# Scaling 16384 tokens by two weights each: smaller tiles, four output buffers, and five of the stores in the ScalarE queue

## The chip, the core and the metric

The kernel runs on one core of a Trainium2 chip. Such a core has compute engines with instruction streams of their own; this kernel computes on VectorE (DVE in the profile) and ScalarE (ACT). SyncE (SP) computes nothing: its stream issues transfers. Data moves between the chip's memory (HBM) and the core's buffer (SBUF, 128 partitions) by 16 DMA engines. They serve two queues here: one is filled by SyncE's stream (q1 in the profile), the other by ScalarE's (q10). The metric is the device time of one execution in microseconds, the median of several runs.

## The reference

```python
batch, seq, hidden, n_experts = 16, 1024, 512, 8
k = 2
x_expanded = x[:, :, np.newaxis, :].repeat(k, axis=2)
weights = expert_weights[..., np.newaxis]
return (x_expanded * weights).astype(np.float32)
```

Every one of the 16 x 1024 = 16384 tokens is a row of 512 fp32 numbers (2 KB). It is written twice, each time multiplied by one of the token's two weights. So 33.6 MB of x are read, 67.1 MB are written, and each number written takes one multiplication. The indices of the experts are not used.

## The kernel before

The tokens are dealt in groups. A group of T tokens per partition takes T x 128 consecutive tokens, and each partition gets T consecutive ones of them (`rows`, L45), so a partition's part of a group is one contiguous piece of memory. `groups` is `[[24], [24], [24], [24], [24], [8]]`, in all the 128 tokens of each partition; each inner number is one tile of x. A tile of 24 tokens has 48 KB in each partition.

The weights come first, in three transfers in SyncE's queue: the first group (L53), the four other groups of 24 (L54), and the group of 8 (L58). A partition's weights of one group of 24 are 24 x 2 fp32 numbers, a row of 192 B; the group of 8 has rows of 64 B.

`load(i)` (L74) issues the load of tile i in ScalarE's queue (L82). The first tile comes in six pieces of 4 tokens (8 KB per partition), every other tile in one transfer. There are two x buffers, so tiles 0 and 1 are loaded ahead, and tile i + 2 is issued by ScalarE's stream after its multiplications of tile i (L119).

The main loop (L90) goes through the tiles, and in each through its tokens and the two weights. An output buffer holds 12 tokens with both copies (48 KB per partition), and there are two of them. Of the products, every third (`c % 3 == 2`) is made on ScalarE (L100), the others on VectorE (L106), each over 128 x 512 numbers, with the weight as one scalar per partition. After every 12 tokens, and at the end of a tile, the output buffer is stored by a transfer in SyncE's queue (L115). All eleven stores are in that queue.

The streams wait by semaphores that the framework sets: a multiplication waits for its tile of x and for the store that last used its output buffer, a store waits for the multiplications that fill its buffer, and a load waits for the multiplications that read its x buffer last. In one stream everything stands in the order of the program: in ScalarE's, the load of tile i + 2 stands between the multiplications of tiles i and i + 1.

Of the kernel before, what the change touches and what calls it, by code (L numbers as in the profile page):

```python
# [1 line left out]

# [4 lines left out]


@with_exitstack
def kernel(  # L10
    ctx: ExitStack,
    tc: tile.TileContext,
    x: bass.AP,
    expert_indices: bass.AP,
    expert_weights: bass.AP,
    out: bass.AP,
):
    nc = tc.nc

    batch, seq, hidden = x.shape  # L20
    k = expert_weights.shape[-1]
    P = nc.NUM_PARTITIONS
    ntok = batch * seq
    assert ntok % P == 0
    A_TOTAL = ntok // P

    f32 = mybir.dt.float32
    row = k * hidden
    TX = 24
    TO = 12  # L30

    groups = [[24], [24], [24], [24], [24], [8]]
    assert sum(sum(g) for g in groups) == A_TOTAL

    xf = x.rearrange("b s h -> (b s) h")
    of = out.rearrange("b s k h -> (b s) (k h)")
    wf = expert_weights.rearrange("b s k -> (b s) k")

    w_pool = ctx.enter_context(tc.tile_pool(name="w_pool", bufs=1))
    x_pool = ctx.enter_context(tc.tile_pool(name="x_pool", bufs=2))  # L40
    o_pool = ctx.enter_context(tc.tile_pool(name="o_pool", bufs=2))

    w_tile = w_pool.tile([P, A_TOTAL * k], f32)

    def rows(of_all, done, T):  # L45
        return of_all[done * P : (done + T) * P, :].rearrange(
            "(p a) n -> p (a n)", a=T
        )

    T0 = sum(groups[0])  # L50
    G = len([g for g in groups[1:] if sum(g) == T0])
    head = (1 + G) * T0
    nc.sync.dma_start(out=w_tile[:, : T0 * k], in_=rows(wf, 0, T0))  # L53
    nc.sync.dma_start(  # L54
        out=w_tile[:, T0 * k : head * k].rearrange("p (g n) -> p g n", g=G),
        in_=wf[T0 * P : head * P, :].rearrange("(g p a) n -> p g (a n)", g=G, p=P),
    )
    nc.sync.dma_start(  # L58
        out=w_tile[:, head * k :], in_=rows(wf, head, A_TOTAL - head)
    )  # L60

    tiles = []
    done = 0
    for group in groups:
        T = sum(group)
        a0 = 0
        for n in group:
            tiles.append((done, T, a0, n))
            a0 += n
        done += T  # L70

    loaded = []

    def load(i):  # L74
        if i >= len(tiles):
            return
        done, T, a0, n = tiles[i]
        x_tile = x_pool.tile([P, TX * hidden], f32)
        src = rows(xf, done, T)
        step = TX // 6 if i == 0 else n  # L80
        for at in range(0, n, step):
            nc.scalar.dma_start(  # L82
                out=x_tile[:, at * hidden : (at + step) * hidden],
                in_=src[:, (a0 + at) * hidden : (a0 + at + step) * hidden],
            )
        loaded.append(x_tile)

    for i in range(2):
        load(i)
    for i, (done, T, a0, n) in enumerate(tiles):  # L90
        x_tile = loaded[i]
        outr = rows(of, done, T)
        for t in range(n):
            if t % TO == 0:
                o_tile = o_pool.tile([P, TO * row], f32)
            for kk in range(k):
                c = (done + a0 + t) * k + kk
                o = t % TO * row + kk * hidden
                if c % 3 == 2:
                    nc.scalar.mul(  # L100
                        out=o_tile[:, o : o + hidden],
                        in_=x_tile[:, t * hidden : (t + 1) * hidden],
                        mul=w_tile[:, c : c + 1],
                    )
                    continue
                nc.vector.tensor_scalar(  # L106
                    out=o_tile[:, o : o + hidden],
                    in0=x_tile[:, t * hidden : (t + 1) * hidden],
                    scalar1=w_tile[:, c : c + 1],
                    scalar2=None,  # L110
                    op0=mybir.AluOpType.mult,
                )
            if (t + 1) % TO == 0 or t + 1 == n:
                at = t // TO * TO
                nc.sync.dma_start(  # L115
                    out=outr[:, (a0 + at) * row : (a0 + t + 1) * row],
                    in_=o_tile[:, : (t + 1 - at) * row],
                )
        load(i + 2)  # L119

# [1 line left out]
_INS = ['x', 'expert_indices', 'expert_weights']  # L122
_OUTS = [((16, 1024, 2, 512), 'float32')]


# [23 lines left out]
```

## Time and profile before

| what | value |
|---|---|
| time, median of 3 runs | 240.6 us (240.56 to 240.91) |
| span of the profiled execution | 238.9 us |
| read from HBM, written to it | 33.69 MB, 67.11 MB |
| load of 24 tokens: size, issue to landing | 6144 KB, 43.9 us (median of 4) |
| store of 12 tokens: size, issue to landing | 6144 KB, 33.6 us (median of 10) |
| one multiplication on VectorE, on ScalarE | 480 ns, 709 ns |

The span goes from the first to the last instruction of the profiled execution; the runs are timed from outside and take in what lies around it. The profile cuts the span in 40 slices; a digit in the row of an engine, or of the DMA engines, is the busy share of that slice in tenths, and 9 stands for 90% or more. A DMA queue's line gives its packets, its megabytes and the time of its packets as a share of the time of 16 engines. A packet is one contiguous row, here the part of one partition in one transfer, and 4 B packets mark the ends of transfers. Lines of waits give who waited for whom: the total in us, how many times, and the longest.

### The profile page before, as it was taken

What the parts mean: (1) busy time and instruction counts of PE and PEld (TensorE: products, weight loads), DVE (VectorE), ACT (ScalarE), POOL (GpSimd) and SP (SyncE); (2) the same over time, 40 slices, a digit from 0 to 9 for tenths busy, and PEclk for the clock granted to TensorE, in tenths of its full rate; (3) what the DMA queues carried; (4) which work ended last, traced back from release to release, by engine and by line L of the source; (5) the groups of instructions that cost most, each with busy time, mean ns of one, the idle gap of its engine ahead of it and who ended that gap; (6) DMA issues with size and microseconds to landing.
All of it is one profiled execution on the core that took longest, in us unless ns stands there. A gap on an engine that the chain in (4) does not pass through costs nothing.

```text
span 238.9 us, 364 instructions
## 1 busy us (share of the span) xinstructions
DVE 69.0 (29%) x171; ACT 54.9 (23%) x86; POOL 0.2 (0%) x4
## 2 busy tenths in 40 slices
DVE  0890300004609100190063037003706406415000
ACT  0870300004308000170071034003406106213000
POOL 0000000000000000000000000000000000000000
DMA  6999999999999999999999999999989899999994
GB/s 244 420 443 395 495 395 395 494 428 395 428 494 395 413 494 411 395 446 469 403 411 502 395 420 453 436 411 428 469 379 496 381 428 469 436 411 428 436 439 197
DMA packets 3986, 100.81 MB, mean 422 GB/s; under 512 B 1168, under 2 KB 1168, under 8 KB 1168
## 3 DMA queue, kind: packets, MB, share of 16 engines
q1 hardware_dynamic: 2400, 67.24, 65.2%
q10 hardware_dynamic: 1584, 33.56, 33.1%
q14 instruction: 2, 0.02, 0.0%
HBM read 33.69 MB, written 67.11 MB: 422 GB/s over the span
## 4 chain that ended last, share of the span: by engine, by line
DMA 66%; DVE 13%; another core or an unknown queue 11%; issue 0%; DVEq 0%; SPq 0%
DMA out_dram<-o_tile 54%; DVE o_tile L106 13%; DMA x_tile<-in_x_dram 11%; DVEq L144 0%; DVEq L106 0%; SPq L115 0%
## 5 line engine op out<-in xcount | busy, mean ns | idle before, releaser
L106 DVE TENSOR_SCALAR o_tile<-x_tile,w_tile 128x512 f32<-128x512 f32 x171 | 69.0, 480 | 149.3 <-DMA out_dram<-o_tile 105.3
L100 ACT ACTIVATE o_tile<-x_tile,w_tile 128x512 f32<-128x512 f32 x85 | 53.6, 709 | 155.5 <-DMA out_dram<-o_tile 116.8
L100 ACT ACT_TABLE_LOAD x1 | 1.3, 1283 | 6.7 <-DMA x_tile<-in_x_dram 6.7
L133 POOL MEMSET const-bfloat16-1.0<- 128x1 bf16 x1 | 0.1, 101 | 0.0
L133 POOL MEMSET const-uint8-127<- 128x1 uint8 x1 | 0.1, 101 | 0.0
L133 POOL MEMSET const-float32-0.0<- 128x1 f32 x1 | 0.1, 98 | 0.2 <-issue 0.2
L133 POOL MEMSET const-float32-1.0<- 128x1 f32 x1 | 0.1, 98 | 0.0
## 6 DMA issues: line engine op xcount, KB each, us to landing
out_dram<-o_tile SPq DMA_DIRECT2D x10, 6144.0 KB, 33.6
x_tile<-in_x_dram ACTq DMA_DIRECT2D x4, 6144.0 KB, 43.9
x_tile<-in_x_dram ACTq DMA_DIRECT2D x6, 1024.0 KB, 10.6
out_dram<-o_tile SPq DMA_DIRECT2D x1, 4096.0 KB, 19.5
x_tile<-in_x_dram ACTq DMA_DIRECT2D x1, 2048.0 KB, 24.0
w_tile<-in_expert_weights_dram SPq DMA_DIRECT2D x1, 96.0 KB, 11.1
w_tile<-in_expert_weights_dram SPq DMA_DIRECT2D x1, 24.0 KB, 2.9
w_tile<-in_expert_weights_dram SPq DMA_DIRECT2D x1, 8.0 KB, 13.2
```

What stands on the lines that cost most here:

```text
L100: nc.scalar.mul(out=o_tile[:, o : o + hidden], in_=x_tile[:, t * hidden : (t + 1) * hidden], mul=w_tile[:, c : c + 1],)
L106: nc.vector.tensor_scalar(out=o_tile[:, o : o + hidden], in0=x_tile[:, t * hidden : (t + 1) * hidden], scalar1=w_tile[:, c : c + 1], scala ...
L133: nc = _bacc.Bacc("TRN2", target_bir_lowering=False, num_devices=1)
```

## The change

- A tile of x has 16 tokens (32 KB per partition) in place of 24; there are still two x buffers. The first tile comes in four pieces of 4 tokens in place of six.
- An output buffer has 8 tokens (32 KB per partition) in place of 12, and there are four of them in place of two. So there are 16 pieces j = 0 to 15 of 8 tokens, and 16 stores in place of 11. The SBUF in use stays at 192 KB per partition and the weights.
- The groups are four of 32 tokens per partition, each cut in two tiles. A partition's rows of x in one group are 64 KB apart from the next partition's, its output rows 128 KB; its weights of a group are a row of 256 B. The weights come in two transfers.
- Pieces 3, 7, 11, 13 and 15 (`beside`) are stored by transfers in ScalarE's queue, the others in SyncE's as before.
- From piece 1 on, the products are dealt by token: the first 4 tokens with both weights are one VectorE operation over 128 x 4096 numbers (x and the weights read with repeats, `to_broadcast`), the last 4 tokens are eight multiplications on ScalarE. Piece 0 is dealt as before.
- `behind()` keeps the instructions of ScalarE's stream behind the transfer issued last in it, so that loads, multiplications and stores there stand in the order of the program: load 2 after piece 1's products, then the products of pieces 2 and 3, store 3, load 3, those of 4 and 5, load 4, those of 6 and 7, store 7, load 5, and so on.

```diff
-    TX = 24
-    TO = 12
+    TX = 16
+    TO = 8
+    XB = 2
+    OB = 4
+    CH = 4
 
-    groups = [[24], [24], [24], [24], [24], [8]]
+    groups = [[16, 16]] * 4
...
-    G = len([g for g in groups[1:] if sum(g) == T0])
-    head = (1 + G) * T0
+    G = len(groups) - 1
     nc.sync.dma_start(out=w_tile[:, : T0 * k], in_=rows(wf, 0, T0))
     nc.sync.dma_start(
-        out=w_tile[:, T0 * k : head * k].rearrange("p (g n) -> p g n", g=G),
-        in_=wf[T0 * P : head * P, :].rearrange("(g p a) n -> p g (a n)", g=G, p=P),
-    )
-    nc.sync.dma_start(
-        out=w_tile[:, head * k :], in_=rows(wf, head, A_TOTAL - head)
+        out=w_tile[:, T0 * k :].rearrange("p (g n) -> p g n", g=G),
+        in_=wf[T0 * P :, :].rearrange("(g p a) n -> p g (a n)", g=G, p=P),
     )
...
+    issued = []
+
+    def behind():
+
+        return tc.issue_after(issued[-1].ins) if issued else ExitStack()
...
-        step = TX // 6 if i == 0 else n
...
+        steps = [4, 4, 4, 4] if i == 0 else [n]
+        for e, step in enumerate(steps):
+            at = sum(steps[:e])
+            with behind():
+                issued.append(
+                    nc.scalar.dma_start(
...
+    S = A_TOTAL // TO
+    beside = [j for j in range(S) if j % 4 == 3 or j == S - 3]
...
+        for at in range(0, n, TO):
+            j = (done + a0 + at) // TO
+            o_tile = o_pool.tile([P, TO * row], f32)
+            for t in range(TO):
+                for kk in range(k if j == 0 or t >= CH else 0):
...
+                    if j > 0 or c % 3 == 2:
+                        with behind():
+                            nc.scalar.mul(
...
+            if j > 0:
+                c = (done + a0 + at) * k
+                nc.vector.tensor_tensor(
+                    out=o_tile[:, : CH * row].rearrange(
+                        "p (t k h) -> p t k h", t=CH, k=k
+                    ),
+                    in0=x_tile[:, at * hidden : (at + CH) * hidden]
+                    .rearrange("p (t h) -> p t h", t=CH)
+                    .unsqueeze(2)
+                    .to_broadcast([P, CH, k, hidden]),
+                    in1=w_tile[:, c : c + CH * k]
+                    .rearrange("p (t k) -> p t k", t=CH)
+                    .unsqueeze(3)
+                    .to_broadcast([P, CH, k, hidden]),
+                    op=mybir.AluOpType.mult,
                 )
...
+            dst = outr[:, (a0 + at) * row : (a0 + at + TO) * row]
+            if j in beside:
+                with behind():
+                    issued.append(nc.scalar.dma_start(out=dst, in_=o_tile))
+            else:
+                nc.sync.dma_start(out=dst, in_=o_tile)
+        load(i + XB)
```

## The prediction, made before the changed kernel was run

> **What bounds the kernel now.** I read the busy table first, then the slices, the DMA queues, the waits, and last the ends of the run in windows of 4 us. The page:
>
> ```profile
> span 238.9 us, 364 instructions
> DVE 69.0 (29%) x171; ACT 54.9 (23%) x86; POOL 0.2 (0%) x4
> DMA  6999999999999999999999999999989899999994
> ...
> DMA packets 3986, 100.81 MB, mean 422 GB/s; under 512 B 1168, under 2 KB 1168, under 8 KB 1168
> q1 hardware_dynamic: 2400, 67.24, 65.2%
> q10 hardware_dynamic: 1584, 33.56, 33.1%
> ```
>
> No compute engine is busy for a third of the span. The packets of the SyncE queue (q1) and of the ScalarE queue (q10) fill 65.2 + 33.1 = 98.3% of the time of 16 DMA engines, 234.8 of 238.9 us; only the first and last slices are under 8 tenths. The waits agree:
>
> ```profile
> ACT o_tile L100 <- DMA out_dram<-o_tile: 116.8, 8, 24.0
> DVE o_tile L106 <- DMA out_dram<-o_tile: 105.3, 8, 22.6
> DVE o_tile L106 <- DMA x_tile<-in_x_dram: 44.0, 6, 27.1
> ```
>
> Both compute engines mostly wait for a store to free an output buffer (total us, times, longest). The chain of waits gives DMA 66% and another 11% to a queue that it could not name. Now the two ends of the run (columns: stretch, length, busy time of the engines, clock, DMA share, GB/s):
>
> ```profile
> 0.00:4.00 4.00, 0.00 (x0) 0.00 (x0) 0.20 (x4) 1.00 0.50 164
> 4.00:8.00 4.00, 2.15 (x6) 1.29 (x2) 0.00 (x0) 1.00 1.04 417
> ...
> 232.00:236.00 4.00, 0.00 (x0) 0.00 (x0) 0.00 (x0) 1.00 0.95 410
> 236.00:238.90 2.90, 0.00 (x0) 0.00 (x0) 0.00 (x0) 1.00 0.03 11
> ```
>
> DMA is at full rate from 4 us to 236 us. The trace's packet records (not on the page) sharpen this: the first packet starts at 1.73 us and the last ends at 237.64; if each packet is chained to the engine that had just come free, no engine stands idle for over 0.3 us at a time after the first 3 us. Where both queues have rows, an engine takes one row of each in turn. So the only things that can change the time are the engine time of all packets, the holes at the two ends, and new holes in the middle.
>
> **The change, part by part, in time of one DMA engine.** A DMA of 128 partitions gives each of the 16 engines 8 rows. Packet records, from start to next start: a 48 KB row 1.812 us, a 32 KB row 1.210 (the 8 rows of the last store), 16 KB 0.608, 8 KB 0.306, a 192 B weight row 0.0117, 64 B 0.0075, the 4 B completion 0.006. Loads and stores cost the same.
>
> Before: 10 stores x 8 x 1.812 = 144.96; the last store 8 x 1.210 = 9.68; 4 loads x 8 x 1.812 = 57.98; the load of 8 tokens 8 x 0.608 = 4.86; 6 first pieces x 8 x 0.306 = 14.69; weights 40 x 0.0117 + 8 x 0.0075 = 0.53; 25 completions 0.15. Sum 232.85.
>
> After: 16 stores x 8 x 1.210 = 154.88; 7 loads x 8 x 1.210 = 67.76; 4 pieces x 8 x 0.306 = 9.79; weights 32 rows of 256 B, which the trace doesn't have (from 64 to 192 B, three times the bytes, a row's time grew by 1.6, so a third more bytes costs nothing to a third more: 0.0117 to 0.0156, together 0.37 to 0.50 us; by the slope 0.0138) 0.45; 29 completions 0.17. Sum 233.05, so **+0.2 us**: more rows of the same bytes. By itself, the 256 B weight row saves 0.1 us.
>
> The ends: before, the profile has 235.9 us from first to last packet against 232.85 of work, so 3.1 us on the engine that ends last. From the records: starting up costs the mean engine 0.4 us, the entry of the first store among the 8 KB loads (15.6 to 17.6 us) 0.7, and the last engine ends 1.1 us behind the mean (236.5), having met two load rows that took 2.47 and 2.33 us in place of 1.81. The change starts with the same 1 MB pieces in the same queue and ends with a 4 MB store again, so I keep all three. The stretch from the last packet to the end of the span, 1.3 us, is kept too, and so is what separates the span from the median of the runs, 240.6 - 238.9 = 1.7.
>
> **Compute is hidden.** A piece of 8 tokens has 8 multiplications on ScalarE (timeline: 8 in 5.01 us) and one on VectorE over 128x4096. VectorE's 128x512 takes 6.42 / 16 = 0.40 us, so 8 times the elements are bounded by 3.2 us (same rate) and 6.4 (half of it, for two full inputs). I take 5.0 to 6.4 us for the piece, ended by whichever is later, against 14.6 us of DMA that each piece brings (233.05 / 16). The Trainium skill, "VectorE: DVE Perf Modes" (section "Mode 2×_2P"), says a fp32 operation on two tensors goes at one element a cycle, where one with a scalar does two; at its 0.96 GHz that is an estimated 4.3 us, inside these bounds, and the sum would not move.
>
> **Holes in the middle.** There are now four output buffers, so up to four stores (4 x 8 x 1.21 = 38.7 us) stand queued. New waits: each ScalarE store (pieces 3, 7, 11, 13, 15) waits for VectorE's part of its piece, and behind it in ScalarE's stream stand the next load's issue and the next multiplications. VectorE's part ends at most 1.4 us after ScalarE's (6.4 - 5.0), so this costs nothing while rows are queued. In the ring, though, load 3 now stands behind store 3, load 5 behind store 7, load 7 behind store 11. A 4 MB transfer takes 9.7 us alone and 19.4 beside another. Worked through row by row with turns taken, load 6 lands near 170 us; then SyncE's ring holds stores 10 and 12 and ScalarE's holds store 11, load 7, store 13. Stores 10 and 11 end near 189, store 12 and load 7 near 208, and store 13 alone covers the next 9.7 us. In them piece 14 must be made and its store must arrive: landing 0.35 (last completion to semaphore, from the trace) + 5.0 to 6.4 + issue 0.33 + 0.6 to the first packet (first load: issue ended 1.14, packet 1.84) = 6.3 to 7.8 us. It fits by 1.9 us or more. Everywhere else at least 16 rows (19.4 us) wait on an engine. SyncE's two DMAs of weights stay ahead of all stores, as now.
>
> **Sum:** 238.9 + 0.2 = 239.1 us span, 240.6 + 0.2 = **240.8 us** for the runs.
>
> **Rivals.**
>
> *Shorter ends* (faster). If the last engine no longer trails the mean, 1.1 us go: 239.7. For it: rows of 32 KB hold up the other ring for 1.2 us rather than 1.8, and the large late rows were only met by chance. Against: without idle time an engine never catches up, whatever the row size. If the 0.7 us at the first store go too: 239.0.
>
> *Hole before store 14* (slower). Its place is the stretch after load 7, from about 208 us; it decides when piece 14's store arrives over 9.7 us after load 7's last row. Before, the first store's issue ended at 13.73 and its first row started at 16.97; with that 3.2 us in place of 0.6 the need is 10.4 us, a hole of 0.7: 241.5. Were store 13 gone already, the whole 6.3 us would show: 247.1. Against: a late start beside a busy ring is the other ring's rows being worked off, no idle time.
>
> *Rows at power-of-two distances* (slower). Groups of 32 put the partitions' x rows 64 KB apart and output rows 128 KB apart, where 24 gave 48 and 96 KB. If memory serves equal low addresses badly, every 32 KB row is stretched. From the trace: the last store's rows lie 32 KB apart and the last load's 16 KB, both powers of two, and both rows lie on the line of the others, so zero from the nearest rows. The far bound is the slowest 48 KB row, 2.47 against 1.81 us, 36% on 222.6 us: about 320. A middle row is the 8 KB loads at the start, mean 0.332 against 0.309, 7%: about 256. The Trainium skill, "DMA: Bandwidth & Descriptors" (section "Latency and other measured facts"), reports this effect, 207 against 214 GB/s at a pitch of 512 KiB and far worse from 2 MiB; no run here shows it, its smallest pitch is four times ours, and its 3.4% would be an estimated 7.6 us here, 248.4.
>
> *The change does not do what it says*: where both rings always hold rows, moving five stores to the other one and 0.2 us more of row time leave no mark: 240.6.
>
> **How the numbers follow.** I take 0.2% (0.5 us, so 240.1 to 241.1) as what a measurement can tell from no change; the three runs shown spread by 0.35. Forecast 0.62 (of it 0.46 inside 0.2%, 0.05 under, 0.11 over, from such fewer or more late rows on the last engine); shorter ends 0.19; hole 0.09; power-of-two rows 0.06; nothing 0.04. Faster 0.05 + 0.19 = 0.24; same 0.46 + 0.04 = 0.50; slower 0.11 + 0.09 + 0.06 = 0.26. The range goes down to 239.5, past the lagging engine's 1.1 us, and up to 242.2, past the hole of 0.7 and as much again of late rows. It leaves out the power-of-two rows (0.06), part of the shorter ends (0.06) and the larger holes (0.04). The forecast's own range is 240.2 to 241.3.
>
> **What would show it.** DMA should stay at 9 tenths in all slices but the ends, the two queues' shares should come to 98% of a span of 239 us, of which ScalarE's takes some 53 (33.56 MB of loads and five stores of 4.19 MB, 54 of 100.8 MB) and SyncE's 45. A 32 KB row over 1.22 us would mean memory; a slice under 9 tenths near 215 us, the hole before store 14; last packet and span closer together with full slices, shorter ends. I am wrong if slices in the middle fall under 8 tenths, or if all are full and the time still moves by over 1 us.

## The result, and the profile after

The changed kernel takes 247.06 us (median of 4 runs, 246.01 to 247.41), the kernel before 240.62 us (median of 4). The ratio is 1.0257, with a 95% interval of 1.0233 to 1.0281: 2.6% slower, 6.4 us, where 0.2 us were forecast. Medians here are over all runs of a kernel, ratios leave disturbed runs out, so the two can differ. Where single runs of an experiment lie far apart, their range is given.

The page of the profile after, the lines that answer to those shown of before:

```profile
span 245.6 us, 272 instructions
DVE 70.3 (29%) x26; ACT 79.0 (32%) x126; POOL 0.2 (0%) x4
DMA  6999999999999999999999999999999999989990
...
DMA packets 4433, 100.80 MB, mean 410 GB/s; under 512 B 976, under 2 KB 976, under 8 KB 976
q10 hardware_dynamic: 2304, 54.53, 53.1%
q1 hardware_dynamic: 2128, 46.27, 43.9%
```

The bytes are the same and both compute engines are still idle for two thirds of the span. The DMA engines look as busy as before, 53.1 + 43.9 = 97.0%, but of a span that is 6.7 us longer: 238.2 us of packets where there were 234.8. Only two slices stand out, an 8 at some 215 to 221 us and the 0 at the end. The waits:

```profile
ACT o_tile L116 <- DMA x_tile<-in_x_dram: 142.0, 10, 31.3
DVE o_tile L131 <- DMA x_tile<-in_x_dram: 135.5, 7, 32.4
```

The compute engines now wait for loads, where they had waited for stores to free buffers: four output buffers moved the wait. That alone costs nothing, as before, while rows are queued.

What a row costs is seen in windows of 9.7 us, the time of eight 32 KB rows. First three neighbours around the start of load 3, then around load 5 and load 7 (columns as before; the last two are DMA share and GB/s):

```profile
60.30:70.00 9.70, 1.40 (x1) 2.40 (x4) 0.00 (x0) 1.00 1.00 432
70.00:79.70 9.70, 0.00 (x0) 0.00 (x0) 0.00 (x0) 1.00 1.03 402
79.70:89.40 9.70, 0.00 (x0) 0.00 (x0) 0.00 (x0) 1.00 1.00 432
...
129.00:138.70 9.70, 0.00 (x0) 0.00 (x0) 0.00 (x0) 1.00 1.00 385
...
188.50:198.20 9.70, 0.00 (x0) 0.00 (x0) 0.00 (x0) 1.00 0.96 385
198.20:207.90 9.70, 0.00 (x0) 0.00 (x0) 0.00 (x0) 1.00 1.00 432
```

The share stays at 1 while the rate falls from 432 to 402 and 385 GB/s: the engines are not idle, their rows take longer. The packet records say which: the median 32 KB row takes 1213 ns, as before, but after 20 us there are 121 rows over 5% longer, most of them while loads 3, 5 and 7 set in, up to 2811 ns. I call them stretched, and such a stretch of time an episode. They cost the mean engine 2.88 us, against 0.21 in the kernel before. They don't fall evenly: by the completions that each DMA engine writes, 13 engines stay within a microsecond of each other, while three fall further behind from load to load. They are 0.8 to 2.7 us behind the median engine at the end of load 3, 2.4 to 3.3 at load 5 and 2.8 to 5.6 at load 7.

Two things follow at the end (timeline, then windows):

```profile
178.43 41.34 SPq L150 DMA_DIRECT2D out_dram<-o_tile  x2
183.34 0.35 ACTq L148 DMA_DIRECT2D out_dram<-o_tile  x1
214.40 9.91 ACT L116 ACTIVATE o_tile<-x_tile,w_tile 128x512 f32<-128x512 f32 x16 [31.10 <-DMA x_tile<-in_x_dram]
214.57 8.76 DVE L131 TENSOR_TENSOR o_tile<-x_tile,w_tile 128x4096 f32<-128x4096 f32 x2 [32.38 <-DMA x_tile<-in_x_dram]
224.34 0.35 ACTq L148 DMA_DIRECT2D out_dram<-o_tile  x1
```
```profile
216.00:220.00 4.00, 4.00 (x2) 4.00 (x8) 0.00 (x0) 1.00 0.70 303
...
236.00:240.00 4.00, 0.00 (x0) 0.00 (x0) 0.00 (x0) 1.00 0.91 393
240.00:244.00 4.00, 0.00 (x0) 0.00 (x0) 0.00 (x0) 1.00 0.10 41
```

Load 7 counts as landed when its last engine is done; ScalarE starts on it at 214.40 us, though the median engine had finished at 208.4. So store 14 is issued only at 219.4 (178.43 + 41.34, less the 0.33 of the issue), and most engines have run out of rows by then: the share falls to 0.70, with holes (idle time of a DMA engine) of 0.8 to 1.5 us on 13 engines. And at the end these 13 are done by 239.9 us, two more by 241.8, and the last one works alone until 244.27.

The sum of the 6.6 us by which the last packet is later (244.27 against 237.64): the median engine ends at 239.8 against 236.3, 3.5 us later, of which 0.2 are the row count, about 1.1 the hole, and the rest, 2.2, stretched rows; the last engine trails the median by 4.5 us against 1.3, another 3.2. With the packets chained to engines as in the prediction, the last engine alone tells it more simply: it has no hole before store 14, and its own stretched rows come to 5.6 us, where those of the last engine before come to 1.2.

### The profile page after: what moved, and what is told of

The parts are those of the page before. It is cut to its first block, busy times and chain, and to the rows that moved or that the text cites. A ratio compares the mean times of both kernels' runs of the same rounds, so it can differ in the third digit from the quotient of the medians.

```text
span 245.6 us, 272 instructions
## 1 busy us (share of the span) xinstructions
DVE 70.3 (29%) x26; ACT 79.0 (32%) x126; POOL 0.2 (0%) x4
## 3 DMA queue, kind: packets, MB, share of 16 engines
q10 hardware_dynamic: 2304, 54.53, 53.1%
q1 hardware_dynamic: 2128, 46.27, 43.9%
## 4 chain that ended last, share of the span: by engine, by line
DMA 54%; another core or an unknown queue 19%; ACT 15%; DVE 2%; ACTq 1%; issue 1%
DMA x_tile<-in_x_dram 38%; DMA out_dram<-o_tile 16%; ACT o_tile L116 15%; DVE o_tile L131 2%; ACTq L89 1%; ACTq L148 0%; ACTq L116 0%
## 5 line engine op out<-in xcount | busy, mean ns | idle before, releaser
L116 ACT ACTIVATE o_tile<-x_tile,w_tile 128x512 f32<-128x512 f32 x125 | 77.7, 708 | 142.0 <-DMA x_tile<-in_x_dram 142.0
L131 DVE TENSOR_TENSOR o_tile<-x_tile,w_tile 128x4096 f32<-128x4096 f32 x15 | 65.7, 4422 | 146.7 <-DMA x_tile<-in_x_dram 135.5
L122 DVE TENSOR_SCALAR o_tile<-x_tile,w_tile 128x512 f32<-128x512 f32 x11 | 4.5, 481 | 6.3 <-DMA x_tile<-in_x_dram 6.3
```

The lines of the kernel that those rows point to most:

```text
L116: nc.scalar.mul(out=o_tile[:, o : o + hidden], in_=x_in, mul=w_tile[:, c : c + 1],)
L122: nc.vector.tensor_scalar(out=o_tile[:, o : o + hidden], in0=x_in, scalar1=w_tile[:, c : c + 1], scalar2=None, op0=mybir.AluOpType.mult,)
L131: nc.vector.tensor_tensor(out=o_tile[:, : CH * row].rearrange("p (t k h) -> p t k h", t=CH, k=k), in0=x_tile[:, at * hidden : (at + CH) * ...
```

## The experiments

Three theories could explain stretched rows, and each has an edit that takes it away. R: a load that stands behind a store in ScalarE's ring (its queue's list of waiting rows) starts badly. P: rows at power-of-two distances collide in memory. D: too many transfers stand queued. A fourth, T, came out of the first runs. Every experiment was compared with the kernel before (240.6 to 240.7 us); "stretched" is the excess of rows over 5% longer than the median of their size after 20 us, per engine, and "trail" is how far the last engine is behind the median at the end. Both are read from the one profiled run of each experiment.

### First round: the store queue and the distances

e1, all stores in SyncE's queue:

```diff
-    beside = [j for j in range(S) if j % 4 == 3 or j == S - 3]
+    beside = []
```

> The changed kernel with all 16 stores in SyncE's queue and none in ScalarE's; pitch, tiles and buffers as changed. Theory R (a load that stands behind a store in the same ring begins with stretched rows, and a few engines never make that up): no load stands behind a store, so no stretched rows beyond the first store's 0.7 us, all engines end within 2 us of each other, 240.5 to 241.5 us. Theory P (rows 64 KB and 128 KB apart, powers of two, are served badly when loads set in): the pitch is unchanged, so rows are still stretched where loads set in among stores, and the time stays over 244 us.

Measured: 243.68 us (three runs from 242.9 to 244.0, one at 248.0), ratio 1.0114 (1.0093 to 1.0136). Stretched 2.09 us, trail 2.6, no hole. Between the two expectations: the store queue accounts for 1.4% of the 2.6, but rows are still stretched, at loads that stand behind loads. R as stated is not the cause of the stretching. The stores ahead of the loads are what makes load 7 late: without them it lands at 182.5 us.

e2, groups that are no power of two:

```diff
-    groups = [[16, 16]] * 4
+    groups = [[16] * 3, [16] * 5]
```

> The changed kernel with groups of 48 and 80 tokens per partition in place of four of 32: x rows 96 and 160 KB apart, output rows 192 and 320 KB, no power of two; the weight rows get 384 and 640 B. Queues, tiles, buffers as changed. Theory P: the stretched rows go and the time comes to 240.5 to 241.5 us. Theory R: loads 3, 5 and 7 still stand behind stores, so 246 to 247.5 us.

Measured: 244.87 us (three runs from 243.8 to 245.1, one at 258.2), ratio 1.0156 (1.0124 to 1.0188). Stretched 2.99 us, no less than in the changed kernel, again at loads 3, 5 and 7; the trail is 2.8 in place of 4.5, and there is no hole. P fails as the cause of the stretching. Three runs are 1.0% faster than the changed kernel, but as the rows are stretched as much, it is not shown that the distance is worth this.

e3 and e4, smaller and larger powers of two (in e4 the second transfer of weights is left out, as one group has them all):

```diff
-    groups = [[16, 16]] * 4
+    groups = [[16]] * 8      (e3)
+    groups = [[16] * 8]      (e4)
```

> The changed kernel with eight groups of 16 tokens per partition: x rows lie 32 KB apart, output rows 64 KB, the powers of two below; weight rows of 128 B. Theory P: a smaller power of two, so less stretch, 241 to 245 us. Theory R: 246 to 247.5 us, as the changed kernel.

> The changed kernel with one group of 128 tokens per partition: x rows 256 KB apart, output rows 512 KB, weights in one transfer with rows of 1024 B. Theory P: a larger power of two, so more stretch than in the changed kernel, 249 us or more. Theory R: 246 to 247.5 us.

Measured: e3 250.14 us with runs from 245.2 to 256.7, ratio 1.0207 (1.0186 to 1.0228); too scattered to rank against the others, but no sign that 32 KB is harmless. In its profiled run, of 256.7 us, 3.99 us are stretched and one DMA engine falls 16 us behind the median. e4: 246.60 us, ratio 1.0254 (1.0201 to 1.0307), the same as the changed kernel at a quarter of the distance; stretched 3.52, more than there, but trail 2.5 and no hole. The time does not grow with the power of two. The Trainium skill, "DMA: Bandwidth & Descriptors" (section "Latency and other measured facts"), gives 207 GB/s at a pitch of 512 KiB against 214 with padded rows. That is an estimated 3.4% and would have put e4 apart from the changed kernel; it isn't, though its output rows lie just that far apart.

### Second round: buffers, sizes and the queue, from both sides

e5 and e6 have two output buffers, e6 also all stores in SyncE's queue; e7 gives the kernel before four buffers of 6 tokens; e8 gives it stores in ScalarE's queue:

```diff
-    OB = 4
+    OB = 2                                   (e5, e6; e6 with beside = [])
-    TO = 12
+    TO = 6                                   (e7, and bufs=4 for o_pool)
-                nc.sync.dma_start(
+                queue = nc.scalar if (done + a0 + at) // TO in (3, 5, 7, 9) else nc.sync
+                queue.dma_start(             (e8)
```

> The changed kernel with two output buffers of 32 KB in place of four; five stores still in ScalarE's queue. Theory D (the load rows are stretched where a load and a store begin together while further transfers stand queued, which four output buffers make possible): at most two stores are outstanding, so the stretches go and the time is 241 to 242.5 us. Theory R/P or none of these (small rows or tiles as such): stretches stay, 244 us or more.

> The changed kernel with two output buffers and all stores in SyncE's queue: of the change only the sizes, the groups and the split of the products are left. Theory D: no stretches after the first store, 240.5 to 241.5 us. If the sizes or the groups do it: 243 us or more, as with four buffers (243.7).

> The kernel before with four output buffers of 6 tokens (24 KB) in place of two of 12; loads of 48 KB rows, groups and queue as before. Theory D: four stores outstanding, and transfers of loads and stores begin together at times, so stretches appear, 242 us or more. Otherwise 240.5 to 241.3 us (only the row count grows).

> The kernel before with the stores 3, 5, 7 and 9 of its eleven moved to ScalarE's queue, ahead of the loads of tiles 3 to 5 there; sizes, two output buffers and groups as before. Theory R (a load behind a store in one ring): stretches at those loads, 242.5 us or more. Theory D: two stores outstanding only, no stretches, 240.5 to 241.5 us unless a later load leaves a hole.

Measured: e5 247.55 us with runs from 245.1 to 251.7, ratio 1.0251 (1.0196 to 1.0305), stretched 6.26 in the run of 251.7; e6 247.09, 1.0262 (1.0232 to 1.0292), stretched 2.93; e7 241.91, 1.0051 (1.0036 to 1.0066), stretched 0.97; e8 248.13, 1.0299 (1.0259 to 1.034), stretched 4.91.

D fails both ways: fewer queued stores did not help (e5, e6), and with all stores in one queue four buffers are better than two (243.7 against 247.1). Smaller stores and four buffers by themselves cost little (e7, though at 0.6 us over what was expected without D and just under what D called for). The sizes, the groups and the split of the products, with the old queue and two buffers, already cost 2.6% (e6); and the store queue alone, with the old sizes, costs 3.0% (e8). So either part is enough, and they don't add: the changed kernel with both, and four buffers, is at 2.6% too.

In e8 the whole length of a load is stretched, stores too. Two pairs of windows of 14.5 us (eight 48 KB rows), of an early load and of the load of tile 4:

```profile
62.90:77.40 14.50, 7.83 (x20) 5.01 (x8) 0.00 (x0) 1.00 1.00 434
77.40:91.90 14.50, 0.00 (x0) 0.00 (x0) 0.00 (x0) 1.00 1.00 434
149.00:163.50 14.50, 6.42 (x16) 5.01 (x8) 0.00 (x0) 1.00 1.05 407
163.50:178.00 14.50, 0.00 (x0) 0.00 (x0) 0.00 (x0) 1.00 0.98 376
```

Same sizes, full engines, 434 GB/s in one place and 376 in another. In the kernel before, windows as long keep nearly the whole rate, though some of its few long rows fall into the first:

```profile
131.60:146.10 14.50, 4.81 (x13) 4.98 (x8) 0.00 (x0) 1.00 0.99 427
62.90:77.40 14.50, 6.27 (x16) 5.01 (x8) 0.00 (x0) 1.00 1.00 434
```

What may differ is how the engines stand to each other. Theory T says that rows are stretched when the engines begin theirs in step. For it: before the three episodes of the changed kernel 9 to 12 of the 16 engines begin their rows within 0.2 us of the median; in e1 from 130 us on only 5 or 6 do, and nearly no row is stretched. Against it: one episode of e1, at 115 to 120 us, also found only 5 that close, and in the kernel before 9 to 12 are that close from 120 us on without an episode. So T is a guess to be tried.

### Third round: spreading the engines

e10 puts four extra loads between the loads of tiles 0 and 1. A transfer of 8, 4, 2 or 1 rows uses only as many DMA engines (its completions show that); if they are the same first ones each time, the first engine gets four rows of 8 KB more than the last eight. Their data is never used. e11 is the same with all stores in SyncE's queue.

```diff
+    load(0)
+    o_tile = o_pool.tile([P, TO * row], f32)
+    for q, e in enumerate((8, 4, 2, 1)):
+        with behind():
+            issued.append(
+                nc.scalar.dma_start(
+                    out=o_tile[:e, q * 2048 : (q + 1) * 2048],
+                    in_=xf[: 4 * e, :].rearrange("(p a) n -> p (a n)", a=4),
+                )
+            )
-    for i in range(XB):
+    for i in range(1, XB):
         load(i)
```

> The changed kernel with four extra loads of 8, 4, 2 and 1 rows of 8 KB between the loads of tiles 0 and 1, into an output buffer that is written again later: they give the first DMA engines up to four rows more than the last, so that the engines no longer begin their rows at the same instant. They add at most 1.2 us of work to one engine. Theory T (engines that start reading at the same instant stretch each other's rows; engines spread over half a microsecond don't): the stretched rows at loads 3, 5 and 7 shrink to less than half, 242 to 245 us. If the tight step of the engines is not what matters: 247 to 248.5 us.

> The same four extra loads with all stores in SyncE's queue. Theory T: from 243.7 us down to 241 to 242.5. If the tight step doesn't matter: 243.7 to 245 us.

Measured: e10 242.22 us, ratio 1.0067 (1.0035 to 1.0099), stretched 0.01 us, trail 1.1; e11 242.90 us, a little over what T called for, ratio 1.0089 (1.007 to 1.0107), stretched 0.23. Of e10's ten runs seven lie from 241.4 to 242.8, one at 245.0 and two at 249.0 and 251.5; the profiled one is the fastest. The windows of e10 over the same three places:

```profile
70.00:79.70 9.70, 0.00 (x0) 0.00 (x0) 0.00 (x0) 1.00 1.00 432
...
129.00:138.70 9.70, 0.00 (x0) 0.00 (x0) 0.00 (x0) 1.00 1.00 432
...
188.50:198.20 9.70, 0.00 (x0) 0.00 (x0) 0.00 (x0) 1.00 1.00 432
```

Not one dip is left in this run, and the hole is gone as well: ScalarE starts on load 7's tile at 207.40 us instead of 214.40. Only 4 of the 16 engines begin their rows within 0.2 us of the median. Distances, queues, buffers and sizes are those of the changed kernel.

```profile
207.40 9.93 ACT L126 ACTIVATE o_tile<-x_tile,w_tile 128x512 f32<-128x512 f32 x16 [28.87 <-DMA x_tile<-in_x_dram]
```

e9 joins the edits of e1 and e2, and e12 gives the kernel before the change's groups (with the third transfer of weights left out, as nothing is left for it):

```diff
-    groups = [[24], [24], [24], [24], [24], [8]]
+    groups = [[24, 8]] * 4                   (e12)
```

> The changed kernel with all stores in SyncE's queue and groups of 48 and 80 tokens per partition: both edits that helped alone, four buffers and small tiles kept. If the store queue (which alone gave back 3.4 us) and the power-of-two distances (2.2 us) are two causes that add, 240.7 to 242 us; if both act on one and the same thing, no better than the better one, 243 us or more.

> The kernel before with four groups of 32 tokens per partition, each a tile of 24 and one of 8: the distances of the change (x rows 64 KB apart, output rows 128 KB) and its 256 B weight rows, with the old output buffers and SyncE's queue for all stores. If power-of-two distances as such cost time: 242.5 us or more. If not: 240.5 to 241.5 us.

Measured: e9 ran at 241.8 us once and at 247.5 to 249.0 three times: not settled. In its profiled run, of 249.0 us, one DMA engine is 8 us behind the median from 190 us to the end, the others within 1.2 us of it: a single engine makes most of the loss. e12 244.91 us, ratio 1.0185 (1.0138 to 1.0231), stretched 2.66. That is the time expected if the distances cost. But the edit also turns six loads into eight that are alternately long and short, so the 1.9% are not shown to be the distance's.

### Fourth round: is it the spread?

e13 has four extra loads of 16 rows each, so every engine gets the same; e14 has e10's with rows of 2 KB; e15 and e16 put e10's into the kernel before and into e8:

```diff
-    for q, e in enumerate((8, 4, 2, 1)):
+    for q, e in enumerate((16, 16, 16, 16)):                (e13)
-                    out=o_tile[:e, q * 2048 : (q + 1) * 2048],
-                    in_=xf[: 4 * e, :].rearrange("(p a) n -> p (a n)", a=4),
+                    out=o_tile[:e, q * 512 : (q + 1) * 512],
+                    in_=xf[:e, :],                          (e14)
```

> As the unequal extra loads (e10), but each of the four extra loads has 16 rows of 8 KB, one for each DMA engine: as many transfers, the same shift of the buffers, no spread between the engines; 4 x 0.306 = 1.2 us of work on every engine. Theory T (the spread of the engines counts): no help, stretched rows at loads 3, 5 and 7 as in the changed kernel, 246.5 to 249 us. If the extra transfers or the shifted buffers helped: 241.5 to 243.5 us.

> As e10, but the extra loads have rows of 2 KB: the engines get up to four rows of 0.08 us, 0.3 us of spread in place of 1.2. Theory T, if a few tenths of a microsecond suffice: 240.6 to 242 us, less than e10 by the work saved. If the spread must be of the size of a row: 244 to 247 us.

> The kernel before with the four unequal extra loads of e10 between its loads of tiles 0 and 1. Theory T: the engines were already spread enough there (few stretched rows), so nothing is won and up to 1.2 us of work on one engine are added, 240.5 to 242 us. If the kernel before loses time to the same thing: under 240.2 us.

> The kernel before with four stores in ScalarE's queue (e8, 248.1 us) and the four unequal extra loads. Theory T: the stretched rows go there too, 241 to 243.5 us. If the store queue costs by itself: 246 us or more.

Measured: e13 251.06 us, ratio 1.0418 (1.0376 to 1.0461), stretched 2.20, trail 4.4. The windows show the dips of the changed kernel again, at some of the same places:

```profile
70.00:79.70 9.70, 0.00 (x0) 0.00 (x0) 0.00 (x0) 1.00 0.98 395
...
188.50:198.20 9.70, 0.00 (x0) 0.00 (x0) 0.00 (x0) 1.00 0.99 395
```

As many transfers, the same shift of buffers, no spread (before the first dip 12 of the 16 engines begin their rows within 0.2 us of the median, in e10 only 4): 8.8 us slower than e10. Its 4.0 us over the changed kernel are about what the extra rows (1.2) and longer 8 and 32 KB rows before 20 us (3.0; 4.15 us of excess per engine there, against 1.12) come to. So in this kernel unequal extra loads remove the stretching in most runs and equal ones don't. That the spread does it is the reading that fits; the equal loads also have more rows, 64 against 15, which no run separates.

e14 ran at 242.4 us once and at 247.8 to 249.1 five times: 0.3 us of spread is not dependable. Its profiled run, of 247.8 us, shows why the mean of stretched rows does not tell the time: it is only 1.12 us, but nearly all of it lies on a few engines. Two of them are nearly 10 us behind the median when load 7 lands, and the hole before store 14 is deeper than in the changed kernel (0.70 there):

```profile
216.00:220.00 4.00, 4.00 (x2) 4.00 (x8) 0.00 (x0) 1.00 0.42 180
```

e15 242.51 us, ratio 1.0091 (1.0063 to 1.0119), stretched 0.28: the kernel before had nothing to win, as expected; it pays 1.9 us, more than the 1.2 at most that the extra rows were expected to cost. e16 252.71 us, ratio 1.0487 (1.0445 to 1.0529), stretched 3.78: T called for 241 to 243.5, and it got slower than e8. There T fails. By its completions the engines of one transfer end up to 15 us apart there after 150 us, so they are far from in step, and the median stretched row of 48 KB takes 2.3 us in place of 1.8.

No version beat the kernel before.

## Why the prediction was wrong

- **What bounds the kernel**, DMA throughout, held before and after. That compute is hidden held too: VectorE's new operation takes 4.42 us (bounds 3.2 to 6.4; the estimate by the Trainium skill, "VectorE: DVE Perf Modes" (section "Mode 2×_2P"), was 4.3), ScalarE's eight 5.0.
- **The row sum** was right in its terms: the median 32 KB row took 1213 ns in all kernels, the queues' shares were forecast at 53 and 45% and came to 53.1 and 43.9. The weights' 256 B rows took 18 ns, 0.56 us in all by their durations against 0.77 before, a saving of 0.2 for the expected 0.1. The three items named for the ends add up to 2.2 of the 3.1 us that they were to explain; the rest was kept without a name.
- **The step that failed** is the one that took every row at its median and the two ends as they were: "an engine never catches up, whatever the row size" was used only against a gain. It also means that every stretched row stays lost. The prediction saw such rows in the trace of before (2.47 and 2.33 us), called them chance and kept their sum. The change raised them from 0.21 to 2.88 us per engine, and on the engine that ends last, where the sum had 1.2, to 5.6. The prediction's own sign of being wrong, full slices and yet over 1 us more, is what came but for one slice.
- **The hole before store 14** was named, at the right place, with its sign (a slice under 9 tenths near 215 us, which came) and its price for one late store (0.7 us); it came to 0.8 to 1.5 us on most engines. The need of 6.3 to 7.8 us was counted from one landing for all engines. Load 7 in fact landed 5.6 us after its median engine, and that is what ate the 9.7 us of cover. The hole did not set the end, since the trailing engine had rows throughout.
- **Power-of-two rows** was the rival that pointed at longer rows, and what it was to show, a 32 KB row over 1.22 us, did show for some rows. As the cause it fell: other distances kept the stretched rows (e2) and a four times larger one was no worse (e4). Whether it takes part is not shown: e2 is 1.0% faster in three of its four runs, with as many stretched rows.
- **Shorter ends** did not come: the last engine trails by 4.5 us, not 1.3.
- The stores in ScalarE's queue were costed at nothing because rows are queued elsewhere. e8 puts them at 3.0% in the kernel before, e1 at 1.4% here.

Open: what holds a row up, and why a few engines lose most. Being in step goes with the episodes of the changed kernel, but it is neither enough (the kernel before from 120 us on) nor needed (e16). The packet records tell when and on how many engines rows are stretched, not what stretches them.

## What to carry to other kernels

A full DMA profile does not say that rows cost what they can cost: compare the rate at a share of 1 between stages, and the completions of single engines, before adding up medians. A transfer lands with its slowest engine, and where engines never idle, one that trails stays behind to the end (8 us for the last 50 us of e9's profiled run), so plan cover for a late landing, not for the median one. In this DMA-bound kernel, tiles with their groups (e6) and the store queue (e8) each cost 2.6 to 3.0% alone without adding a byte, so measure each alone, and in several runs, since two versions ran 6 us apart from run to run (e9, e14).

## What the runs showed of the hardware that was not expected

- Equal rows in equal transfers ran at 434 or at 376 GB/s within one execution (e8), with the DMA engines busy in both.
- A few rows of 8 KB that were dealt unequally to the DMA engines at 13 us kept all later rows but one near their median for 220 us in the profiled run, and took 4.8 us off the median of the changed kernel (e10; two of ten runs were slower than it); dealt equally they added 4.0 (e13). In the kernel before with a second store queue, the unequal ones added 4.6 us (e16 against e8).
- The Trainium skill, "DMA: Bandwidth & Descriptors" (section "Issuing engines are not separate DMA queues"), says that issuing from several engines saves issue time only. The runs agree that it wins no bandwidth, and show that it can cost: 7.4 us (e8).
